# Sixteen down-projection tiles with the low part's first tokens appended to the high part's matmul

## The chip, the core and the metric

The kernel runs on one core of one Trainium2 chip. The metric is the device time of one execution in microseconds (us), the median of several runs; less is better.

## The reference

One inference step of a two-layer decoder trunk over 256 prompt tokens and 8 sample tokens (264 token columns), model width 2048, all in float32. Layer 0 mixes tokens with a Conformer convolution module, layer 1 with a gated linear recurrence (HGRN2); behind each mixer stands a channel mixer, and a last RMSNorm closes it. The change lies in the channel mixer of layer 0:

```python
def conv_ffn(x, buf, w_up, w_dw, b_dw, w_down):
    h = x @ w_up                                        # 2048 -> 2 * 5632
    h, new_buf = causal_depthwise_conv(h, buf, w_dw, b_dw)
    gate, up = jnp.split(h, 2, axis=-1)
    return (jax.nn.silu(gate) * up) @ w_down, new_buf   # 5632 -> 2048
...
        x = x + y
        h = rmsnorm(x, norm_ffn[i])
        y, s = conv_ffn(h, ffn_state[i], ffn_w_up[i], ffn_w_dw[i], ffn_b_dw[i], ffn_w_down[i])
        x = x + y
```

## The kernel before

Channels lie on the 128 partitions and the T = 264 tokens along the free axis. A product is computed in output tiles of 128 channels. TensorE holds a 128x128 weight block, streams the 128x264 activations of one block of input channels past it, and adds up over the k blocks in one PSUM bank (512 float32 per partition).

Nearly all products are done in three passes. The weights are cut by ScalarE into a high part `wh` and by VectorE into a low part `wl`, the activations likewise into a high and a low part, all of type float32r (the page prints it as f32 on TensorE); what is added up is high by high, `wh` by low, and `wl` by high. That is `step`: three matmuls of 264 columns for each k, at L179 (`wh`, high), L180 (`wh`, low) and L181 (`wl`, high). Each loads its own weight block. A product that is on the list `NATIVE` is done instead in plain float32 by one instruction for each k (L176), which the trace records as two matmuls.

The work is cut into slots, written out by hand and in a fixed order: `slot` issues the matmuls of one output tile on TensorE, and then what goes along with it on VectorE and ScalarE: work put off by `later` (the previous tile's addition to the residual stream `x` in `residual`, L278; the gating and convolution of up-projection tiles) and the split of the weights two tiles ahead (`split_hi` L137, `split_lo` L149). Weight tiles are loaded by DMA further ahead still; the raw weights, `wh` and `wl` have three buffers each, PSUM tiles five.

`conv_ffn` cuts the 5632 hidden channels into `CHUNKS` = 4 chunks of `FC` = 11 blocks of 128. For a chunk, `up` computes 22 up-projection tiles (16 blocks deep, so 48 matmuls each), and gates them into `gh` and `gl`, the high and the low part of 11 activation blocks; `down` computes 16 down-projection tiles `p_dn` (11 blocks deep, 33 matmuls each), and each is added to `x`. A chunk's down tiles run behind the next chunk's up tiles, except for the last chunk, whose down tiles follow at once. So the first chunk's down tiles of layer 0, 16 tiles and 528 matmuls, run from 611.3 to 675.8 us, between up-projection tiles.

Inside a down slot the second matmul reads `gl`, which VectorE has written as `gate - gh` (L587), long before.

Of the kernel before, what the change touches and what calls it, by code (L numbers as in the profile page):

```python
# [17 lines left out]
P = 128  # L18
# [13 lines left out]

# columns of the packed per-channel parameters
_FIELDS = [
# [8 lines left out]

# output tiles of the first two products that go through the four-pass float32 path
NATIVE = {("pw1", n) for n in range(2 * KT)} | {("pw2", 0), ("pw2", 1), ("ho", 0)}
AHEAD = 2
LOADS = 4
TE = 17
# the second mixer's products: gates wait, so that enough of them are left to stream beside the last head's scan
GATE_AFTER = (3, 4, 6, 7, 9, 10, 12, 13, 15)  # L50
# [10 lines left out]
def kernel(ctx: ExitStack, tc: tile.TileContext, a: dict):  # L61
# [11 lines left out]

# [1 line left out]
    xall = cp.tile([P, KT, T], F32, tag="x", name="x")  # L75
# [12 lines left out]

# [1 line left out]
    order = []  # L90
# [64 lines left out]

# [1 line left out]
    todo = [([], [], []) for _ in range(12)]  # L157

    def later(slots, fn, last=False, first=False):
        """Run fn in the slots-th slot from here: before the split of a coming weight tile, or after it."""  # L160
        todo[slots][0 if first else 2 if last else 1].append(fn)
# [10 lines left out]

    def step(pt, ww, k, last, rhs, full):
        wh, wl = ww
        if wl is None:
            pe.matmul(pt[:, :T], wh[:, k, :], full[k], start=(k == 0), stop=last)  # L176
            return
        rh, rl = rhs[k]
        pe.matmul(pt[:, :T], wh[:, k, :], rh, start=(k == 0), stop=False)  # L179
        pe.matmul(pt[:, :T], wh[:, k, :], rl, start=False, stop=False)  # L180
        pe.matmul(pt[:, :T], wl[:, k, :], rh, start=False, stop=last)  # L181

    def slot(keys, rhs, full=None, ahead=AHEAD):
        """One product (or a few, side by side) and the work that goes along with it."""
        upto("hi", split_hi, cnt["use"] + len(keys))
        upto("lo", split_lo, cnt["use"] + len(keys))
        pts = []
        for key in keys:
            assert order[cnt["use"]] == key, (order[cnt["use"]], key)
            cnt["use"] += 1  # L190
            pts.append((bank(f"p_{key[0]}_{key[1]}"), parts.pop(key)))
        upto("load", load, cnt["use"] - 1 + LOADS)
        for k in range(depth(keys[0])):
            for pt, ww in pts:
                step(pt, ww, k, k == depth(keys[0]) - 1, rhs, full)
        begin, early, late = turn()
        for fn in begin:
            fn()
        upto("hi", split_hi, cnt["use"] + ahead)
        for fn in early:  # L200
            fn()
        upto("lo", split_lo, cnt["use"] + ahead)
        for fn in late:
            fn()
        return [pt for pt, _ in pts]

# [1 line left out]
    def rsqrt_steps(y, v, t):  # L208
        """y = v ** -0.5 by Newton steps from a guess on the exponent's bits."""
        yi = y.bitcast(I32)  # L210
        yield vec.tensor_scalar(out=yi, in0=v.bitcast(I32), scalar1=1, scalar2=None, op0=ALU.arith_shift_right)
        yield vec.tensor_scalar(out=yi, in0=yi, scalar1=-1.0, scalar2=float(0x5F3759DF), op0=ALU.mult, op1=ALU.add)
        for _ in range(3):
            yield vec.tensor_tensor(out=t, in0=v, in1=y, op=ALU.mult)
            yield vec.scalar_tensor_tensor(out=t, in0=t, scalar=-0.5, in1=y, op0=ALU.mult, op1=ALU.mult)
            yield vec.scalar_tensor_tensor(out=y, in0=t, scalar=1.5, in1=y, op0=ALU.add, op1=ALU.mult)
# [5 lines left out]
    class Stats:  # L222
        """Sum of squares over the channels, a tile at a time; then 1/rms on every partition."""

# [46 lines left out]

    def residual(n, pt, st, hl, name, scale, bias=None):
        """x += product, in the next slot; and what the next product needs of it."""
        hold = {}

        def add():
            if bias is None:
                vec.tensor_tensor(out=x[n], in0=x[n], in1=pt[:, :T], op=ALU.add)  # L278
            else:
                vec.scalar_tensor_tensor(out=x[n], in0=pt[:, :T], scalar=bias, in1=x[n], op0=ALU.add, op1=ALU.add)  # L280
            if st is not None:
                hold["sq"] = st.square(x[n])
            if hl is not None:
                hl.append(high(n, x[n], name, scale(n)))
            elif st is not None:
                act.activation(x[n], x[n], AF.Identity, scale=pcol("norm_final", n))
# [9 lines left out]

    # lower bounds of the forget gates: softmax over the layers' axis, cumulated, less the first
    lb = cp.tile([P, KT], F32, tag="lb", name="lb")
# [13 lines left out]

    # ================= layer 0, mixer: Conformer convolution =================
    with ExitStack() as ph:
# [63 lines left out]

        # the last tile: TE of its taps on the tensor engine, as products with diagonal matrices
        diag = {}  # L380
# [14 lines left out]
        def taps(i, lo, hi):  # L395
            """Two sums, of every other tap: c[i], which the last tap opened, and part, with what is independent of it."""
            u, ci = m[i], c[i]
# [132 lines left out]

    # ================= channel mixer =================
    def conv_ffn(layer, hl, rs, scale):
        """scale: what the next product's operand is scaled with (None: no product follows)."""
        rstd = rs.y
        with ExitStack() as ph:
# [39 lines left out]
            def up(f):  # L575
                gh = fp.tile([P, T], F32R, tag="gh", name=f"gh{layer}_{f}", bufs=2 * FC)
                gl = fp.tile([P, T], F32R, tag="gl", name=f"gl{layer}_{f}", bufs=2 * FC)
                cg = half(f, "g")
# [7 lines left out]
                later(1, gate)  # L586
                later(1, lambda: vec.tensor_tensor(out=gl, in0=cu, in1=gh.bitcast(F32), op=ALU.subtract), last=True)  # L587
                return gh, gl

# [3 lines left out]
            def down(ch, g):  # L593
                end = ch == CHUNKS - 1
                for n in range(KT):
                    pt, = slot([(f"dn{layer}", ch * KT + n)], g)
                    residual(n, pt, st if end else None, nxt if end else None, f"after{layer}", scale)

# [13 lines left out]

    # ================= layer 1, mixer: HGRN2 =================
    with ExitStack() as ph:
# [11 lines left out]
        o2 = h1.tile([P, HEADS, T], F32, tag="o2", name="o2")  # L626
        # what a pair of neighbouring blocks of b tokens is scaled with: queries by (1, the first's gates), keys by (the second's, 1)
        G = {}
# [4 lines left out]
        def gated_by(b):  # L633
            """The gates of all blocks of b tokens, in their order."""
            at = G[b][:, 0, 0, 1:]
            n = SEQ // (2 * b)
            return bass.AP(at.tensor, at.offset, [at.ap[0], [2, n], [2 * n - 1, 2]])
# [28 lines left out]
        def doubling(h, lo, hi):  # L666
            """Products of the gates to a block's end, times the keys, and from its start, times the queries; it doubles."""
            d = heads[h]
# [36 lines left out]

        # the layer norm's 1/rms with tokens on partitions
        rtok = h1.tile([P, 3], F32, tag="rtok", name="rtok")
# [111 lines left out]
        def sample_state_and_norm(h):  # L819
            """By turns: neither waits for its last step, then."""  # L820
            for _ in zip_longest(sample_state(h), head_norm(h)):
                pass
# [31 lines left out]

        # the samples' norms: of all heads but the last, and of the last
        def sample_squares(lo, hi):
# [34 lines left out]
        def parted(last):  # L891
            """The output of the heads up to here in two parts, in buffers that the scan is done with."""
            lo, hi = len(ohl), last + 1
# [61 lines left out]

    # ================= final norm: the prompt's with tokens on partitions =================
    with ExitStack() as ph:
# [13 lines left out]
        for i in range(2):  # L971
            turn_back(i, 0, bank(f"p_y{i}_0"))
        # sums of squares: of the prompt's tokens on their partitions, of the samples' on every partition
        for i in range(3):
# [120 lines left out]
```

## Time and profile before

| what | before |
|---|---|
| median of 3 runs | 2487.59 us (2486.34 to 2487.78) |
| span of the profiled execution | 2484.5 us |
| TensorE matmul busy | 2460.8 us, 99% of the span |
| VectorE busy | 1762.4 us, 71% |
| ScalarE busy | 1109.1 us, 45% |
| mean granted TensorE clock | 0.997 |
| HBM traffic | 182 GB/s over the span |

How to read it: the profiled execution is given by its span, from the first to the last instruction of the core; the run list holds no time for that execution apart, and the median lies 3.1 us above the span, which is what lies around it (start and end of a launch). PE is TensorE's matmuls, PEld its weight loads, which run beside matmuls; DVE is VectorE and ACT is ScalarE. A matmul's duration in the rows runs from its start to a modelled end and overlaps the next matmul's; the distance from one start to the next is what a matmul costs.

### The profile page before, as it was taken

How to read it: one execution, taken by the hardware profiler on the slowest of the kernel's cores; microseconds unless marked ns; L12 is line 12 of the kernel's file. 1: busy time of each engine (PE TensorE's matmuls, PEld its weight loads, DVE VectorE, ACT ScalarE, POOL GpSimd, SP SyncE). 2: the span in 40 equal slices, each digit the busy share in tenths (PEclk: the TensorE clock that was granted, in tenths of full speed). 3: DMA queues.
4: the chain of work that ended last, by engine and by line, in shares of the span. 5: the costliest groups of instructions: out<-in, count | busy, mean ns of one | idle time of the engine just before them, and what ended most of it. 6: DMA issues, size and time to landing. Idle time of an engine off the chain costs nothing.

```text
span 2484.5 us, 46787 instructions
## 1 busy us (share of the span) xinstructions
PE 2460.8 (99%) x19879; PEld 2411.7 (97%) x19879; DVE 1762.4 (71%) x3098; ACT 1109.1 (45%) x1743; POOL 0.2 (0%) x4
## 2 busy tenths in 40 slices
PE   8999899999999999999999999999999999999998
PEld 7888899999999999999999999999999999999998
DVE  8999867676576566568877777767676656656655
ACT  1112645444344344345655565444444444434434
POOL 0000000000000000000000000000000000000000
PEclk9999999999999999999999999999999999999999
DMA  7443445544644554555555555455555455465453
GB/s 268 151 153 141 170 174 200 186 175 159 205 176 161 196 187 166 181 188 203 211 187 199 201 211 191 161 202 193 187 175 182 157 201 185 152 205 187 161 178 129
DMA packets 78129, 452.92 MB, mean 182 GB/s; under 512 B 8544, under 2 KB 13024, under 8 KB 39008
## 3 DMA queue, kind: packets, MB, share of 16 engines
q1 hardware_dynamic: 77920, 449.94, 51.4%
q8 instruction: 155, 2.54, 0.4%
q14 instruction: 54, 0.44, 0.0%
HBM read 436.31 MB, written 15.50 MB: 182 GB/s over the span
## 4 chain that ended last, share of the span: by engine, by line
PE 99%; DVE 1%; DMA 0%; ACT 0%; issue 0%; SPq 0%; ACTq 0%; DVEq 0%
PE p_up L181 14%; PE p_up L179 14%; PE p_up L180 14%; PE p_pw L176 10%; PE p_dn L181 7%; PE p_dn L180 7%; PE p_dn L179 7%; PE p_hi L179 1%; PE p_hf L179 1%; PE p_hq L179 1%; PE p_hf L181 1%; PE p_hi L180 1%; PE p_hq L181 1%; PE p_hi L181 1%; PE p_hq L180 1%; PE p_hf L180 1%
## 5 line engine op out<-in xcount | busy, mean ns | idle before, releaser
L179 PE MATMUL p_up<-h_ffn,wh_up 128*128 128x264 f32 x2816 | 801.0, 284 | 0.0
L181 PE MATMUL p_up<-h_ffn,wl_up 128*128 128x264 f32 x2816 | 800.7, 284 | 0.0
L180 PE MATMUL p_up<-l_ffn,wh_up 128*128 128x264 f32 x2816 | 797.6, 283 | 0.0
L149 DVE TENSOR_TENSOR wl_up<-w_up,wh_up 128x2048 fp32r<-128x2048 f32 x176 | 403.6, 2293 | 231.9 <-ACT wh_up L137 231.9
L137 ACT CAST wh_up<-w_up 128x2048 fp32r<-128x2048 f32 x176 | 335.9, 1909 | 505.7 <-PE p_up L180 446.8
L179 PEld LDWEIGHTS p_up<-h_ffn,wh_up 128*128 128x128 f32 x2816 | 530.1, 188 | 0.1
L181 PEld LDWEIGHTS p_up<-h_ffn,wl_up 128*128 128x128 f32 x2816 | 530.0, 188 | 0.0
L180 PEld LDWEIGHTS p_up<-l_ffn,wh_up 128*128 128x128 f32 x2816 | 529.7, 188 | 0.1
L181 PE MATMUL p_dn<-gh,wl_dn 128*128 128x264 f32 x1408 | 400.8, 285 | 0.0
L179 PE MATMUL p_dn<-gh,wh_dn 128*128 128x264 f32 x1408 | 400.3, 284 | 0.0
L180 PE MATMUL p_dn<-gl,wh_dn 128*128 128x264 f32 x1408 | 400.1, 284 | 0.0
L137 ACT CAST wh_dn<-w_dn 128x1408 fp32r<-128x1408 f32 x128 | 175.9, 1374 | 325.9 <-PE p_dn L180 243.8
L149 DVE TENSOR_TENSOR wl_dn<-w_dn,wh_dn 128x1408 fp32r<-128x1408 f32 x128 | 208.1, 1625 | 108.3 <-ACT wh_dn L137 108.3
L180 PEld LDWEIGHTS p_dn<-gl,wh_dn 128*128 128x128 f32 x1408 | 265.3, 188 | 0.0
L181 PEld LDWEIGHTS p_dn<-gh,wl_dn 128*128 128x128 f32 x1408 | 264.7, 188 | 0.0
L179 PEld LDWEIGHTS p_dn<-gh,wh_dn 128*128 128x128 f32 x1408 | 264.6, 188 | 0.0
L176 PE MATMUL p_pw<-xg,w_pw 128*128 128x264 f32 x960 | 213.9, 386 | 0.0
L176 PEld LDWEIGHTS p_pw<-xg,w_pw 128*128 128x128 f32 x960 | 182.4, 190 | 31.2
L567 DVE SCALAR_TENSOR_TENSOR C<-H,par,C 128x255 f32<-128x255 f32 x352 | 169.2, 481 | 6.3
L278 DVE TENSOR_TENSOR x<-x,p_dn 128x264 f32<-128x264 f32 x128 | 54.9, 429 | 111.9 <-PE p_dn L181 111.9
L561 DVE TENSOR_TENSOR H<-p_up,rstd_ffn 128x264 f32<-128x264 f32 x176 | 76.0, 432 | 78.2 <-PE p_up L181 78.2
L562 ACT ACTIVATE C<-H,par 128x264 f32<-128x264 f32 x176 | 105.5, 599 | 13.9 <-DVE H L561 13.9
(307 smaller groups left out, 4047.8 us busy)
## 6 DMA issues: line engine op xcount, KB each, us to landing
w_up<-in_up SPq DMA_DIRECT2D x176, 1024.0 KB
w_dn<-in_dn SPq DMA_DIRECT2D x128, 704.0 KB
w_pw<-in_pw SPq DMA_DIRECT2D x47, 1024.0 KB
w_hf<-in_hf SPq DMA_DIRECT2D x16, 1024.0 KB
w_hq<-in_hq SPq DMA_DIRECT2D x16, 1024.0 KB
w_hi<-in_hi SPq DMA_DIRECT2D x16, 1024.0 KB
w_hg<-in_hg SPq DMA_DIRECT2D x16, 1024.0 KB
w_ho<-in_ho SPq DMA_DIRECT2D x16, 1024.0 KB
```

What stands on the lines that cost most here:

```text
L137: act.copy(wh[:, :kk, :], raw[key][:, :kk, :])
L149: vec.tensor_tensor(out=wl[:, :kk, :], in0=raw.pop(key)[:, :kk, :], in1=wh.bitcast(F32)[:, :kk, :], op=ALU.subtract)
L176: pe.matmul(pt[:, :T], wh[:, k, :], full[k], start=(k == 0), stop=last)
L179: pe.matmul(pt[:, :T], wh[:, k, :], rh, start=(k == 0), stop=False)
L180: pe.matmul(pt[:, :T], wh[:, k, :], rl, start=False, stop=False)
L181: pe.matmul(pt[:, :T], wl[:, k, :], rh, start=False, stop=last)
L278: vec.tensor_tensor(out=x[n], in0=x[n], in1=pt[:, :T], op=ALU.add)
L561: vec.tensor_tensor(out=h, in0=pt[:, :T], in1=rstd, op=ALU.mult)
L562: act.activation(cc, h, AF.Identity, scale=wv[:, j, 2:3], bias=pcol("ffn_b", layer * 2 * FT + j))
L567: vec.scalar_tensor_tensor(out=cc[:, d:SEQ], in0=h[:, : SEQ - d], scalar=wv[:, j, 2 - d : 3 - d], in1=cc[:, d:SEQ], op0=ALU.mult, op1=ALU.add)
```

## The change

Of the 16 down tiles of chunk 0 in layer 0 (`WIDE_AT`), the first 8 get a width of 400, the last 8 of 512. `gh` and `gl` of one block now lie side by side in one tile `gb` of 528 columns, everywhere in both channel mixers. For a wide tile, the first matmul of each k streams the first `wide` columns of `gb` past `wh`: all 264 of the high part, and the first 136 (or 248) of the low part, whose products land in PSUM columns 264 and up. The second matmul is `wl` by the high part, as the third was before. The third is `wh` by the rest of the low part, 128 (or 16) columns, added onto PSUM columns 136 (or 248) to 263. The columns streamed for each k stay 792, and each k still has three matmuls, each with its own weight load. In `residual`, a second VectorE addition brings the products of PSUM columns 264 and up to `x`.

```diff
+WIDE = [400] * 8 + [512] * 8
+WIDE_AT = (0, 0)
...
-    def step(pt, ww, k, last, rhs, full):
+    def step(pt, ww, k, last, rhs, full, wide=0):
...
+        if wide:
+            both = rhs[k][2]
+            pe.matmul(pt[:, :wide], wh[:, k, :], both[:, :wide], start=(k == 0), stop=False)
+            pe.matmul(pt[:, :T], wl[:, k, :], both[:, :T], start=False, stop=False)
+            pe.matmul(pt[:, wide - T : T], wh[:, k, :], both[:, wide:], start=False, stop=last)
+            return
-        rh, rl = rhs[k]
+        rh, rl = rhs[k][:2]
...
                 vec.tensor_tensor(out=x[n], in0=x[n], in1=pt[:, :T], op=ALU.add)
+                if wide:
+                    rest = slice(0, wide - T)
+                    vec.tensor_tensor(out=x[n][:, rest], in0=x[n][:, rest], in1=pt[:, T:wide], op=ALU.add)
...
-                gh = fp.tile([P, T], F32R, tag="gh", name=f"gh{layer}_{f}", bufs=2 * FC)
-                gl = fp.tile([P, T], F32R, tag="gl", name=f"gl{layer}_{f}", bufs=2 * FC)
+                gb = fp.tile([P, 2 * T], F32R, tag="gb", name=f"gb{layer}_{f}", bufs=2 * FC)
+                gh, gl = gb[:, :T], gb[:, T:]
...
-                    pt, = slot([(f"dn{layer}", ch * KT + n)], g)
-                    residual(n, pt, st if end else None, nxt if end else None, f"after{layer}", scale)
+                    wide = WIDE[n] if (layer, ch) == WIDE_AT else 0
+                    pt, = slot([(f"dn{layer}", ch * KT + n)], g, wide=wide)
+                    residual(n, pt, st if end else None, nxt if end else None, f"after{layer}", scale, wide=wide)
```

What stands on TensorE at the start of the first down tile, two of its eleven k: before,

```order
L179 MATMUL p_dn0_0_5615<-gh0_0_2705,wh_dn0_0_5536 128x264
L180 MATMUL p_dn0_0_5615<-gl0_0_2706,wh_dn0_0_5536 128x264
L181 MATMUL p_dn0_0_5615<-gh0_0_2705,wl_dn0_0_5545 128x264
L179 MATMUL p_dn0_0_5615<-gh0_1_2843,wh_dn0_0_5536 128x264
L180 MATMUL p_dn0_0_5615<-gl0_1_2844,wh_dn0_0_5536 128x264
```

and now, where the first of each three is 400 columns wide, `wl` has moved from third place to second, and 128 columns are left for the third:

```order
L184 MATMUL p_dn0_0_5593<-gb0_0_2705,wh_dn0_0_5514 128x400
L185 MATMUL p_dn0_0_5593<-gb0_0_2705,wl_dn0_0_5523 128x264
L186 MATMUL p_dn0_0_5593<-gb0_0_2705,wh_dn0_0_5514 128x128
L184 MATMUL p_dn0_0_5593<-gb0_1_2842,wh_dn0_0_5514 128x400
L185 MATMUL p_dn0_0_5593<-gb0_1_2842,wl_dn0_0_5523 128x264
```

In both, the three matmuls of one k alternate between two weight blocks, so no two neighbours share one. From tile 8 on the widths are 512, 264 and 16.

What stands on VectorE in the same place (additions to `x`, splits of coming weight tiles into `wl`, the last `gl` of the second chunk): before,

```order
L278 TENSOR_TENSOR x_69<-x_69,p_dn0_0_5615 128x264
L149 TENSOR_TENSOR wl_dn0_3_5706<-w_dn0_3_5616,wh_dn0_3_5698 128x1408
L587 TENSOR_TENSOR gl0_21_5484<-C0_65_5614,gh0_21_5483 128x264
L278 TENSOR_TENSOR x_69<-x_69,p_dn0_1_5662 128x264
L149 TENSOR_TENSOR wl_dn0_4_5748<-w_dn0_4_5663,wh_dn0_4_5745 128x1408
```

and now:

```order
L288 TENSOR_TENSOR x_69<-x_69,p_dn0_0_5593 128x264
L291 TENSOR_TENSOR x_69<-x_69,p_dn0_0_5593 128x136
L153 TENSOR_TENSOR wl_dn0_3_5685<-w_dn0_3_5594,wh_dn0_3_5676 128x1408
L600 TENSOR_TENSOR gb0_21_5462<-C0_65_5592,gb0_21_5462 128x264
L288 TENSOR_TENSOR x_69<-x_69,p_dn0_1_5640 128x264
L291 TENSOR_TENSOR x_69<-x_69,p_dn0_1_5640 128x136
```

One addition of 136 (later 248) columns stands behind each of 16 others and ahead of the split of a coming weight tile; nothing else has moved.

More of the change, by code (lines that the diff above doesn't have):

```diff
@@ L181, in step, with slot @@
         pe.matmul(pt[:, :T], wl[:, k, :], rh, start=False, stop=last)
-    def slot(keys, rhs, full=None, ahead=AHEAD):
+    def slot(keys, rhs, full=None, ahead=AHEAD, wide=0):
         upto("hi", split_hi, cnt["use"] + len(keys))
@@ L194, in slot @@
             for pt, ww in pts:
-                step(pt, ww, k, k == depth(keys[0]) - 1, rhs, full)
+                step(pt, ww, k, k == depth(keys[0]) - 1, rhs, full, wide)
         begin, early, late = turn()
@@ L270, in low, with residual @@
         return h, lo
-    def residual(n, pt, st, hl, name, scale, bias=None):
+    def residual(n, pt, st, hl, name, scale, bias=None, wide=0):
         hold = {}
@@ L586, in up @@
                 later(1, gate)
-                later(1, lambda: vec.tensor_tensor(out=gl, in0=cu, in1=gh.bitcast(F32), op=ALU.subtract), last=True)
-                return gh, gl
+                later(1, lambda: vec.tensor_tensor(out=gl, in0=cu, in1=gb.bitcast(F32)[:, :T], op=ALU.subtract), last=True)
+                return gh, gl, gb
             st = Stats(f"after{layer}", apart=scale is None)
```

## The prediction

> **What bounds the kernel now.** I read the page from the top: the engines' busy time, then the chain that ended last, then TensorE's own waits, and last the stretch in which the changed tiles run.
>
> ```profile
> span 2484.5 us, 46787 instructions
> PE 2460.8 (99%) x19879; PEld 2411.7 (97%) x19879; DVE 1762.4 (71%) x3098; ACT 1109.1 (45%) x1743; POOL 0.2 (0%) x4
> PE 99%; DVE 1%; DMA 0%; ACT 0%; issue 0%; SPq 0%; ACTq 0%; DVEq 0%
> PE p_pw L176 <- DMA w_pw<-in_pw: 7.3, 1, 7.3
> PE p_pw L176 <- ACT c L512: 6.8, 1, 6.8
> PE p_taps L393 <- DVE u L372: 1.2, 1, 1.2
> PE p_y L967 <- ACT y L995: 1.0, 1, 1.0
> ```
>
> TensorE is the bound: 99% of the chain is its matmuls, and its waits for others are the four rows quoted, 16.3 us together (engine and line, what it waited for, us in total, times, the longest). The first three lie in layer 0's mixer, ahead of the changed tiles; only the last, 1.0 us in the final norm, lies behind them. So a microsecond that TensorE gains or loses in the down tiles has next to nothing to be absorbed in, and reaches the end.
>
> The stretch itself, by time windows (start and end, length, busy time and count; granted clock, DMA share, GB/s; the first row is the tile `p_dn` on PE alone, the second all engines, PE, PEld, DVE, ACT, POOL):
>
> ```profile
> 611.33:675.75 64.42, 64.42 (x528) 1.00 0.56 189
> 611.30:676.00 64.70, 64.70 (x532) 64.70 (x531) 35.73 (x38) 24.45 (x21) 0.00 (x0) 1.00 0.56 190
> ```
>
> 528 matmuls in 64.42 us: 122.0 ns from one to the next, without a gap, at a granted clock of 1.00. Three of them, one k of one tile, cost 366.0 ns. VectorE works 35.73 us of 64.70, ScalarE 24.45, DMA is at 0.56.
>
> **What a matmul of another width costs.** Everything hangs on what those 122.0 ns consist of: time that goes with the columns, a fixed part, or the weight load that runs beside it. The timeline at the start of the stretch (start us, duration us):
>
> ```profile
> 611.33 0.29 PE L179 MATMUL p_dn<-gh,wh_dn 128*128 128x264 f32 x1
> 611.33 0.19 PEld L180 LDWEIGHTS p_dn<-gl,wh_dn 128*128 128x128 f32 x1
> 611.46 0.28 PE L180 MATMUL p_dn<-gl,wh_dn 128*128 128x264 f32 x1
> 611.46 0.19 PEld L181 LDWEIGHTS p_dn<-gh,wl_dn 128*128 128x128 f32 x1
> 611.58 0.28 PE L181 MATMUL p_dn<-gh,wl_dn 128*128 128x264 f32 x1
> ```
>
> The weights of the next matmul start to load when the matmul before it starts to stream, and not earlier: one weight block is loaded ahead, no more. So a matmul costs the longer of its own streaming and the load of its successor's weights, and I need both prices.
>
> *The load.* The nearest rows are the plain float32 products of one column, where nothing streams, and some others:
>
> ```profile
> 1187.18:1188.97 1.79, 1.79 (x16) 1.00 0.78 183
> L798 PEld LDWEIGHTS pos<-qks,sm x256: 190/192/192, 1187.0 to 1591.3; 128*128 128x128 f32 x128
> L739 PEld LDWEIGHTS pl<-R x640: 138/138/138, 1157.0 to 1561.7; 128*64 128x64 f32 x160
> L180 PEld LDWEIGHTS p_dn<-gl,wh_dn 128*128 128x128 f32 x1408 | 265.3, 188 | 0.0
> ```
>
> In the first row (L798 alone) 16 matmuls of one column follow each other every 1.79 / 16 = 0.112 us: that is the load of 128 weight columns. The recorded load time (the middle one of min/median/max) follows the weight columns, 192 ns for 128 and 138 for 64, and is 188 in the float32r down tiles. So I take it that a float32r block loads as slowly as a float32 one: 112 ns. Lower is not likely by more than those 4 ns; higher it can't be than 122, since the 264-column matmuls keep that pace.
>
> *The streaming.* Plain float32 has rows of other widths (each record streams twice, in two passes):
>
> ```profile
> L176 PE MATMUL p_pw<-xg,w_pw 128*128 128x264 f32 x960 | 213.9, 386 | 0.0
> L393 PE MATMUL p_taps<-u,diag 128*128 128x226 f32 x2 | 0.5, 354 | 0.0
> 99.73 1.08 PEld L176 LDWEIGHTS p_pw<-xg,w_pw 128*128 128x128 f32 x5
> ```
>
> From 226 to 264 columns the duration grows by 386 - 354 = 32 ns, 0.842 ns a column for two passes, 0.421 for one. Five loads of those products take 1.08 us, the last of them 0.19: (1.08 - 0.19) / 4 = 222.5 ns each, which is 264 x 0.842 = 222.3 with nothing fixed on top, the 112 ns load hidden beneath. For float32r, 264 x 0.421 = 111.1 ns, and measured are 122.0: 10.9 ns more. No row has float32r of another width, so these 10.9 ns are bounded. Low end: they come only because streaming and load are equally long there (111 and 112 ns) and disturb each other, and a wide matmul is free of them. High end: they go with the columns, 122.0 / 264 = 0.462 ns each. I take the value between, 10.9 ns fixed for each matmul that streams longer than its successor loads, since neither row decides.
>
> The Trainium skill, "TensorE: Matmul & The Clock Gate", section "Back-to-back issue gap", puts the distance of matmuls at N/2.4 + 2.5 ns at the full clock. By that the 264-column matmul would take 112.5 ns; the trace has 122.0, so the measurement decides here, and with 169.2 and 215.8 ns for the wide ones the sum would be that of the low end.
>
> **The sum.** One k before: 3 x 122.0 = 366.0 ns. After, in the new order: a wide matmul (beneath it the load of `wl`), 264 columns of `wl` (beneath it the load of `wh`; 122.0 as now), and a narrow one, 128 or 16 columns, whose streaming of 54 or 7 ns is shorter than the load of the next k's `wh`, so it costs 112.
>
> - 400 wide: 400 x 0.421 + 10.9 = 179.3; 179.3 + 122.0 + 112 = 413.3 ns, +47.3.
> - 512 wide: 215.6 + 10.9 = 226.5; 226.5 + 122.0 + 112 = 460.5 ns, +94.5.
> - 8 tiles of 11 k each: 88 x (47.3 + 94.5) ns = 12.5 us.
> - Low end: 168.4 and 215.6 for the wide ones, 402.4 and 449.6 ns: 88 x (36.4 + 83.6) = 10.6 us.
> - High end: 0.462 a column, 184.8 and 236.5, and 122.0 for the narrow ones, 428.8 and 480.5 ns: 88 x (62.8 + 114.5) = 15.6 us.
>
> In one sentence: the columns are the same 792, but the long matmul has nothing to hide for its last 60 to 110 ns, and the short one no longer hides a load.
>
> **The rest costs nothing, and this is the cover:**
>
> ```profile
> 612.81 1.63 DVE L149 TENSOR_TENSOR wl_dn<-w_dn,wh_dn 128x1408 fp32r<-128x1408 f32 x1 [0.85 <-ACT wh_dn L137]
> L278 DVE TENSOR_TENSOR x<-x,p_dn 128x264 f32<-128x264 f32 x128 | 54.9, 429 | 111.9 <-PE p_dn L181 111.9
> L569 DVE TENSOR_TENSOR C<-C,pre 128x8 f32<-128x8 f32 x176 | 28.1, 160 | 0.0
> ```
>
> The 16 second additions: between 160 ns for 8 columns and 429 for 264, so 295 for 136 and 412 for 248, 8 x 0.295 + 8 x 0.412 = 5.7 us on VectorE, which idles 64.70 - 35.73 = 29 us in this stretch. Behind each waits the split of a coming weight tile. The one at 612.81 us is for the third tile and is done at 614.44; that tile starts two tiles later, 611.33 + 2 x 33 x 0.122 = 619.4. So a delay of 0.4 us meets a margin of 5.0, and slower tiles widen it. That `wl` is needed one matmul earlier takes 0.1 us from the same margin; that `wh` is read to the tile's last matmul frees its buffer 0.1 us later, against ScalarE's idle 40 us here. The PSUM tile is held 0.4 us longer, of five. Laying `gh` and `gl` in one tile adds no instruction; every block is finished a whole chunk of up tiles before its down tiles, or 16 down tiles before in the last chunk. DMA: the same transfers, in a stretch that gets longer.
>
> So the profiled span would go from 2484.5 to 2497.0, and the median, 3.1 us above the span, from 2487.6 to 2500.1. A measurement of this kernel can tell about 0.2% (5.0 us) from no change; +12.5 is 0.5%.
>
> **Rivals.**
>
> *Not slower: loads run further ahead.* If TensorE could fetch two weight blocks ahead, the idle 60 to 110 ns beneath the wide matmul would take up the load of the third. Then only columns and fixed parts count, 792 x 0.421 + 3 x 10.9 = 366 ns as before: 0 us, 2487.6. If the disturbance went too, loads alone would bound, 3 x 112 = 336: -30 ns x 176 = -5.3 us, 2482.3. It decides from the point where the narrow matmul costs less than about 65 ns beside 400 and 17 beside 512. For it: nothing in the rows. Against it: in the timeline each load starts with the preceding matmul and not before. The Trainium skill's same section speaks for it: for a sustained stream of load and matmul it gives 81 ns at N=128 and 131 at N=512, with loads pulled ahead through the queue. By that the three would cost what three of 264 cost; the 112 ns of the one-column row contradicts the 81.
>
> *Narrow float32r is slower.* All float32r rows have 264 columns; a matmul of 128 or 16 might need more passes.
>
> ```profile
> L798 PE MATMUL pos<-qks,sm 128*128 128x1 f32 x256 | 29.5, 245 | 0.0
> ```
>
> Plain float32 does: 16 heads of 8 one-column products, 128, stand as 256 records, so 2 x 112 = 224 ns each. Were all narrow ones done so, 112 ns more on 176 of them: 19.7 us on top, +32.2, 2519.8. Were they streamed four times with one load, 128 columns would take 4 x 128 x 0.421 = 215.6, 16 columns stay under the load: 88 x 103.6 ns = 9.1 on top, +21.6, 2509.2. Against it: plain float32 keeps its price per column from 264 down to 226 without a step.
>
> *VectorE's second addition is not covered.* Then a tile start waits for it: 5.7 us on top, +18.2, 2505.8. Against it the 5.0 us margin.
>
> **How the numbers follow.** Load-bound narrow matmuls as summed: 0.76. Narrow ones dearer still: 0.13, of which 0.08 for the cheaper form. Addition uncovered: 0.04. Loads further ahead: 0.07, of which 0.05 no change and 0.02 faster. The time is the first case's, 2500.1. Its own bounds are 2498.2 to 2503.2; down to 2495.5 it has room for a load of 108 and a little more, and the range goes up to 2510 to take in the uncovered addition and the cheaper form of dear narrow matmuls: 0.71 + 0.04 + 0.07. Slower is 0.76 + 0.13 + 0.04 = 0.93, same 0.05, faster 0.02.
>
> **What would show it.** In the profile after, the stretch from 611.3 us should hold the same 528 matmuls in about 64.4 + 12.5 = 76.9 us: 8 tiles of 4.55 us (11 x 413.3) and 8 of 5.07 (11 x 460.5). The load behind a narrow matmul and that matmul should be 112 ns apart from the next load, and loads beneath wide ones should come early and wait. If the stretch still takes 64 us, loads run ahead; if the 128-column tiles are slower than the 16-column ones, or records double, narrow float32r is dear; if PE shows waits for `wl_dn` or `x`, the additions cost. All other stretches should keep their length; a change there would mean that the joined tile `gb` matters, which I have at nothing.

## The result, and the profile after

The changed kernel takes 2500.59 us (median of 3, 2500.38 to 2500.84) against 2487.59: 13.0 us or 0.5% slower, ratio 1.0054, 95% interval 1.0034 to 1.0074. Its profiled execution has a span of 2498.6 us. The page, the changed stretch by time windows (the whole, all engines; then the 8 tiles of width 400 and the 8 of width 512 on PE alone), and PE's waits:

```profile
span 2498.6 us, 46803 instructions
PE 2474.9 (99%) x19879; PEld 2423.1 (97%) x19879; DVE 1768.0 (71%) x3114; ACT 1109.1 (44%) x1743; POOL 0.2 (0%) x4
PE 99%; DVE 1%; DMA 0%; ACT 0%; issue 0%; SPq 0%; ACTq 0%; DVEq 0%
611.64:689.03 77.39, 77.39 (x530) 73.58 (x529) 41.17 (x52) 24.21 (x20) 0.00 (x0) 1.00 0.48 160
611.64:648.26 36.62, 36.62 (x265) 1.00 0.45 146
648.26:689.03 40.77, 40.77 (x266) 1.00 0.50 173
PE p_pw L180 <- DMA w_pw<-in_pw: 7.3, 1, 7.3
PE p_pw L180 <- ACT c L525: 6.8, 1, 6.8
PE p_taps L406 <- DVE u L385: 1.2, 1, 1.2
PE p_y L981 <- ACT y L1009: 1.0, 1, 1.0
```

TensorE still carries 99% of the chain, with the same number of records (19879) and the same four waits, now at other line numbers. The 16 tiles take 77.39 us where they took 64.42: the 13.0 us are here. A tile of width 400 takes 36.62 / 8 = 4.58 us and one of 512 takes 5.10, where 4.55 and 5.07 were forecast. PEld is no longer busy throughout (73.58 of 77.39): beneath the long matmuls it has nothing to do. The granted clock is 1.00 as before.

Where inside a k, the timeline shows (start us, duration us): a 400-wide tile above, a 512-wide one below.

```profile
614.32 0.28 PE L185 MATMUL p_dn<-gb,wl_dn 128*128 128x264 f32 x1
614.32 0.19 PEld L186 LDWEIGHTS p_dn<-gb,wh_dn 128*128 128x128 f32 x1
614.44 0.22 PE L186 MATMUL p_dn<-gb,wh_dn 128*128 128x128 f32 x1
614.44 0.19 PEld L184 LDWEIGHTS p_dn<-gb,wh_dn 128*128 128x128 f32 x1
614.50 0.39 PE L184 MATMUL p_dn<-gb,wh_dn 128*128 128x400 f32 x1
614.55 0.19 PEld L185 LDWEIGHTS p_dn<-gb,wl_dn 128*128 128x128 f32 x1
614.73 0.28 PE L185 MATMUL p_dn<-gb,wl_dn 128*128 128x264 f32 x1
...
653.77 0.17 PE L186 MATMUL p_dn<-gb,wh_dn 128*128 128x16 f32 x1
653.77 0.19 PEld L184 LDWEIGHTS p_dn<-gb,wh_dn 128*128 128x128 f32 x1
653.79 0.48 PE L184 MATMUL p_dn<-gb,wh_dn 128*128 128x512 f32 x1
653.88 0.19 PEld L185 LDWEIGHTS p_dn<-gb,wl_dn 128*128 128x128 f32 x1
654.11 0.28 PE L185 MATMUL p_dn<-gb,wl_dn 128*128 128x264 f32 x1
```

Here one has to read the load rows, not the matmul rows. The wide matmul behind a narrow one is recorded early (614.50, or 653.79), but its weights began to load only at 614.44 (653.77) and it can't stream before they are there: its record is longer by the wait (478 ns on average for 512 columns, against 396 in the swapped order below, where the wide matmul doesn't wait). As in the prediction's timeline, a load starts when the matmul before its own starts to stream, so the distance from one load to the next is what the matmul in between really costs. Averaged over the 88 k of each width (start to start of the loads, ns):

```
                     wide    264 columns   narrow    sum     before
400 / 264 / 128      186.8      121.6       108.3    416.7    366.1
512 / 264 / 16       234.6      120.9       108.2    463.7    366.1
```

88 x (50.6 + 97.6) ns = 13.0 us. A narrow matmul costs 108 ns whether it has 128 columns or 16.

### The profile page after: what moved, and what is told of

It is laid out like the page before. It is cut to its first block, busy times and chain, and to the rows that moved or that the text cites. A ratio compares the mean times of both kernels' runs of the same rounds, so it can differ in the third digit from the quotient of the medians.

```text
span 2498.6 us, 46803 instructions
## 1 busy us (share of the span) xinstructions
PE 2474.9 (99%) x19879; PEld 2423.1 (97%) x19879; DVE 1768.0 (71%) x3114; ACT 1109.1 (44%) x1743; POOL 0.2 (0%) x4
## 4 chain that ended last, share of the span: by engine, by line
PE 99%; DVE 1%; DMA 0%; ACT 0%; issue 0%; SPq 0%; ACTq 0%; DVEq 0%
PE p_up L191 14%; PE p_up L189 14%; PE p_up L190 14%; PE p_pw L180 10%; PE p_dn L189 6%; PE p_dn L191 6%; PE p_dn L190 6%; PE p_dn L184 2%; PE p_hi L189 1%; PE p_hf L189 1%; PE p_hq L189 1%; PE p_hf L191 1%; PE p_hq L191 1%; PE p_hi L190 1%; PE p_hi L191 1%; PE p_hq L190 1%
## 5 line engine op out<-in xcount | busy, mean ns | idle before, releaser
L189 PE MATMUL p_dn<-gb,wh_dn 128*128 128x264 f32 x1232 | 353.9, 287 | 0.0
L191 PE MATMUL p_dn<-gb,wl_dn 128*128 128x264 f32 x1232 | 350.1, 284 | 0.0
L190 PE MATMUL p_dn<-gb,wh_dn 128*128 128x264 f32 x1232 | 350.1, 284 | 0.0
L190 PEld LDWEIGHTS p_dn<-gb,wh_dn 128*128 128x128 f32 x1232 | 233.5, 190 | 0.0
L191 PEld LDWEIGHTS p_dn<-gb,wl_dn 128*128 128x128 f32 x1232 | 232.9, 189 | 0.0
L189 PEld LDWEIGHTS p_dn<-gb,wh_dn 128*128 128x128 f32 x1232 | 231.3, 188 | 0.0
```

## The experiments

Six kernels were run, each beside runs of the kernel before on the same chip (its medians there were 2487.09 and 2486.81 us). Theory L is the prediction's: a narrow matmul costs its successor's weight load, a wide one its streaming, the rest is free.

**Only the joined tile.**

```diff
-WIDE = [400] * 8 + [512] * 8
+WIDE = [0] * 16
```

> Only the layout of the change is left: high and low part lie in one joined tile, every down tile runs as three matmuls of 264 columns as before. Theory L (a narrow matmul costs the 109 ns load of its successor's weights, the rest of the change is free): no change, within 1 us of the kernel before, 2487.6 us. Rival J (the joined tile costs): part of the 13 us stays, 3 us or more above before.

Measured 2488.02 us, ratio 1.0003 (0.9994 to 1.0011). The stretch, tile `p_dn` on PE:

```profile
611.72:676.14 64.42, 64.42 (x528) 1.00 0.56 189
```

64.42 us, as before: in the changed tiles the layout costs nothing. Elsewhere it costs a little. The later down tiles of layer 0, chunk 1 and then chunks 2 and 3 together, all with three matmuls of 264 columns, before and below it with the joined tile:

```profile
804.39:868.71 64.32, 64.32 (x528) 1.00 0.55 190
997.35:1126.10 128.75, 128.75 (x1056) 1.00 0.56 188
```

```profile
804.77:869.30 64.53, 64.53 (x528) 1.00 0.55 189
997.93:1126.89 128.96, 128.96 (x1056) 1.00 0.56 188
```

Each of these two stretches is 0.21 us longer, and so are the same two of layer 1: 0.8 us in all, which the spread of the runs hides from the medians. The changed kernel has the same lengths there (64.54 and 128.96). What makes the difference was not tried.

**All down tiles 288 wide.**

```diff
-WIDE = [400] * 8 + [512] * 8
-WIDE_AT = (0, 0)
+WIDE = [288] * 16
+WIDE_AT = [(l, c) for l in range(2) for c in range(CHUNKS)]
...
-                    wide = WIDE[n] if (layer, ch) == WIDE_AT else 0
+                    wide = WIDE[n] if (layer, ch) in WIDE_AT else 0
```

> All 128 down tiles of both layers 288 wide, so 240 columns for the third matmul: everything of the change but the narrow matmul, eight times as often. Theory L: the third matmul streams 240 x 0.46 = 111 ns, just above the 109 ns load, so the three cost 366 ns as before: within 3 us of before, 2485 to 2491 us. Rival J (the cost comes with the wide form as such): the change's 13 us times 8, about 2590 us; in part, if in part.

Measured 2487.1 us, ratio 1.0000 (0.9991 to 1.0009), and in the first chunk:

```profile
612.13:676.58 64.45, 64.45 (x528) 1.00 0.57 189
```

The whole form of the change (the new order of the three matmuls, overlapping accumulation in PSUM, the second addition, 128 of them) stands in this kernel eight times over, and costs nothing as long as the third matmul has 240 columns. Rival J is out: the form doesn't cost the 13 us, the widths do. The second additions have only 24 columns here, so the prediction's rival of an uncovered addition is settled elsewhere: in the changed kernel TensorE has no wait for `x`, `p_dn` or `wl_dn` among its four, and the 400-wide tiles of the half-weights kernel below, with additions of 136 columns, take the time before.

**A ladder of widths.** The same places, and

```diff
-WIDE = [400] * 8 + [512] * 8
+WIDE = [272 + 16 * n for n in range(16)]
```

> The sixteen tiles of each of the eight chunks get sixteen widths, 272 to 512 in steps of 16 (narrow ones of 256 down to 16 columns): a price list. Theory L: the narrow one costs its own streaming, 0.46 ns a column, down to 236 columns (109 ns), and 108 to 109 flat below; wide ones grow with the columns, 125 to 235 ns. So the three cost 366 ns as before up to a width of 288, then 0.46 ns more for every column. Sum over the widths 750 ns for one k of all sixteen, times 88: 66 us above before (60 to 75), 2548 to 2563 us. Rival J (joined tile, second addition, earlier use of the low weights cost): extra time at 272 and 288 too. Rival N (narrow float32r is dear below some width): a jump at that width.

Measured 2552.07 us, ratio 1.0263 (1.0244 to 1.0281): 65.3 us. Seven of the sixteen tiles of the first chunk, of widths 272, 288, 304, 320, 336, 400 and 512 (a window of one tile is one row; 4.03 us was a tile before):

```profile
611.42:615.43 4.01, 4.01 (x33) 1.00 0.14 52
615.43:619.45 4.02, 4.02 (x35) 1.00 0.49 179
619.45:623.56 4.11, 4.11 (x35) 1.00 0.54 175
623.56:627.72 4.16, 4.16 (x35) 1.00 0.53 177
627.72:631.97 4.25, 4.25 (x35) 1.00 0.54 175
645.19:649.76 4.57, 4.57 (x35) 1.00 0.43 154
678.75:683.86 5.11, 5.11 (x36) 1.00 0.60 202
```

Free at 272 and 288, then every 16 columns cost more. The distances of the loads over all eight chunks (ns), for seven wide matmuls and the narrow one of each (of the narrow ones without the last k of a tile):

```
wide      272    288    304    320    336    400    512
costs   125.8  134.5  142.9  149.7  157.6  186.5  234.4
narrow    256    240    224    208    192    128     16
costs   117.3  110.2  108.6  108.6  108.6  108.5  108.4
```

The narrow price falls with the columns down to 240 and is flat at 108.3 to 109.4 for all fourteen widths from 224 to 16. There is no jump anywhere, so the rival of dear narrow float32r (N) is out. Wide matmuls grow by (234.4 - 125.8) / 240 = 0.4525 ns a column.

**The narrow matmul beside the same weights.** In the changed kernel's 16 tiles, the last two of the three change places:

```diff
             pe.matmul(pt[:, :wide], wh[:, k, :], both[:, :wide], start=(k == 0), stop=False)
-            pe.matmul(pt[:, :T], wl[:, k, :], both[:, :T], start=False, stop=False)
-            pe.matmul(pt[:, wide - T : T], wh[:, k, :], both[:, wide:], start=False, stop=last)
+            pe.matmul(pt[:, wide - T : T], wh[:, k, :], both[:, wide:], start=False, stop=False)
+            pe.matmul(pt[:, :T], wl[:, k, :], both[:, :T], start=False, stop=last)
```

> The changed tiles with the order wide, narrow, 264 columns of the low weights: now wide and narrow use the same weight block one after the other. Theory L, each matmul loads its own block and only one block ahead: the narrow matmul again covers the next load (now of the low weights) badly, the same 13 us above before, 2500.6 us. Rival S, an equal block is not loaded again, or loads run ahead by two: the load of the low weights starts beneath the wide matmul, and the cost is 0 to 3 us, 2488 to 2491 us. In the trace L has 108 to 109 ns from the narrow matmul's successor's load to the next load.

Measured 2500.76 us, ratio 1.0056 (1.0042 to 1.0070), the change's own time. The loads of one k of a 512-wide tile, and the first load of the next:

```profile
655.11 0.19 PEld L184 LDWEIGHTS p_dn<-gb,wh_dn 128*128 128x128 f32 x1
655.24 0.19 PEld L185 LDWEIGHTS p_dn<-gb,wh_dn 128*128 128x128 f32 x1
655.47 0.19 PEld L186 LDWEIGHTS p_dn<-gb,wl_dn 128*128 128x128 f32 x1
655.58 0.19 PEld L184 LDWEIGHTS p_dn<-gb,wh_dn 128*128 128x128 f32 x1
```

From the load of `wl` to the next load are 108.4 ns on average behind the 400-wide matmuls and 108.6 behind the 512-wide ones. The narrow matmul's block equals the one in use, and still has a load of its own (L185), as long in the record as the others. The load of `wl` (L186) does not start beneath the wide matmul, although nothing else is loaded there for over 70 ns. This is the prediction's rival of loads that run further ahead, and it is out.

**Half the weights behind the narrow matmul.** On top of the swapped order:

```diff
-            pe.matmul(pt[:, :T], wl[:, k, :], both[:, :T], start=False, stop=last)
+            m = P if last else 64
+            pe.matmul(pt[:m, :T], wl[:, k, :m], both[:, :T], start=False, stop=last)
```

> As the swapped order, but in ten of eleven k the low weights' matmul takes only 64 of the 128 weight columns (half of that product is left out), still streaming 264 columns. So the matmul that follows the narrow one has half the weights to load. Theory L: the narrow one costs 54 ns in place of 108 (the load of 64 columns by the float32 rows), 160 x 54 ns = 8.7 us less than the swapped order, 2491.9 us. Rival O (108 ns is a narrow float32r matmul's own least time, whatever loads beside it): the same as the swapped order, 2500.6 us.

Measured 2491.85 us, ratio 1.0021 (1.0012 to 1.0030): 8.9 us under the swapped order. Its 400-wide and 512-wide tiles, below those of the swapped order, and a piece of its timeline:

```profile
612.08:648.72 36.64, 36.64 (x265) 1.00 0.45 148
648.72:689.72 41.00, 41.00 (x265) 1.00 0.48 170
```

```profile
611.61:643.84 32.23, 32.23 (x264) 1.00 0.49 164
643.84:680.57 36.73, 36.73 (x265) 1.00 0.56 193
```

```profile
655.30 0.17 PE L185 MATMUL p_dn<-gb,wh_dn 128*128 128x16 f32 x1
655.31 0.14 PEld L187 LDWEIGHTS p_dn<-gb,wl_dn 128*64 128x64 f32 x1
655.33 0.32 PE L187 MATMUL p_dn<-gb,wl_dn 128*64 128x264 f32 x1
655.36 0.19 PEld L184 LDWEIGHTS p_dn<-gb,wh_dn 128*128 128x128 f32 x1
```

The same narrow matmul of 16 columns, with 64 weight columns to load behind it, now costs 55.3 ns (80 k; 655.31 to 655.36), where it cost 108.6. With 128 columns it costs 58.9, a little more: there its own streaming has become the longer. So 108 ns was never the narrow matmul's own time (rival O is out); it is the load of 128 weight columns, and 55 that of 64. The 400-wide tiles are back at 32.23 us, the time before, since in ten of eleven k hardly any load is left uncovered there.

**Without the narrow matmul.** The third `pe.matmul` line of the wide form is dropped, and `stop=last` moves to the second.

> The narrow matmul is left out (the high weights by the last 128 or 16 low columns of the 16 changed tiles are missing from the sum). Theory L: its whole 108 ns go and nothing else: a wide matmul of 186.8 or 234.6 and one of 121.5 ns remain, 308 and 356 ns against 366 before: 88 x (58 + 10) = 6.0 us below before, 2481.6 us. If wide matmuls delay what comes behind them by more than their own streaming, as they would if the accumulation of overlapping columns were what costs, it is less of a gain, or none.

Measured 2479.76 us, ratio 0.9972 (0.9961 to 0.9983). The two halves of the stretch, again on PE:

```profile
610.94:637.55 26.61, 26.61 (x176) 1.00 0.60 198
637.55:668.38 30.83, 30.83 (x178) 1.00 0.64 221
```

57.44 us, 7.0 less than before, where I expected 6.0: the wide matmuls cost 181.4 and 230.7 ns here, against 186.8 and 234.6 in the changed kernel. So the wide matmul that follows a load-bound narrow one is itself 4 to 5 ns dearer. The swapped order points the same way: there the 264-column matmul follows the narrow one and costs 124.3 in place of 121.2, while the wide one falls to 183.4 and 233.3. A small delay, then, seems to fall on whichever matmul comes behind a wait for weights. Its size is uncertain by some 2 ns and its cause was not tried: in the joined kernel's first chunk, where nothing waits, the first, second and third matmul of a k average 123.4, 122.0 and 120.6 ns.

## Why the prediction was right

- *The bound and where the time shows.* TensorE's time reached the end undiminished: 13.0 us in the stretch, 13.0 between the medians. The profiled span grew by 14.1: besides the 13.0 there are 0.8 us in the later down tiles, which the joined tile alone brings too and the prediction had at nothing, and 0.3 ahead of the stretch, whose start lies anywhere from 610.94 to 612.13 us in the eight traces. So it is in part chance that the medians differ by the stretch's 13.0 alone; the three runs of the kernel before spread over 1.4 us.
- *One load ahead, so a short matmul costs the next load.* Right, and shown three ways: flat price from 224 columns down, no load ahead in the swapped order, and half the price for half the weights.
- *The load: taken at 112 ns, measured 108.3.* I took the pace of the one-column float32 products and set the 4 ns between the recorded load times (192 and 188) aside; the measured price is lower by nearly as much: 176 x 3.7 ns = 0.7 us too much. The Trainium skill, "TensorE: Matmul & The Clock Gate", section "LDWEIGHTS (loading the stationary operand)", gives a load as its columns divided by 1.2, 106.7 ns for 128 and 53.3 for 64, whatever the rows; the trace's 108.4 and 55.3 lie 2 ns above both.
- *The streaming: 10.9 ns fixed taken, of bounds from none to 0.462 ns a column.* This was the term most off: the wide ones cost 186.8 and 234.6, not 179.3 and 226.5, 1.4 us too little, and at the high end of what I had for 400 columns, even 2 ns above it. Of that, 4 to 5 ns are the delay behind a narrow matmul, which the sum did not have. What is left, 181.4 and 230.7 in the kernel without the narrow matmul, grows by 0.44 ns a column, and from 264 columns on by 0.43 to 0.45, as one compares with the joined kernel's 123.4 or with the 121.0 and 119.6 beside the wide ones. That is more than the 0.421 that the prediction took from plain float32, so the surplus goes partly with the columns.
- *The 264-column matmul: 122.0 taken, 121.6 and 120.9 measured*, 0.1 us.
- The two larger errors have opposite signs, 1.4 - 0.7 - 0.1 = 0.6 us, which is why 12.5 came so near to 13.0. The time was better than its terms.
- *The additions and waits at nothing.* Right: 296 and 411 ns each (295 and 412 had been put between two rows), beneath VectorE's idle time, no new wait on PE, and the 400-wide tiles with half the weights take the time before (32.23 against 32.21 us) with the same additions.

```profile
L291 DVE TENSOR_TENSOR x<-x,p_dn 128x248 f32<-128x248 f32 x8 | 3.3, 411 | 0.3
L291 DVE TENSOR_TENSOR x<-x,p_dn 128x136 f32<-128x136 f32 x8 | 2.4, 296 | 0.3
```

## What to carry to other kernels

With as many matmuls and columns as before, moving columns from one matmul to another wins next to nothing here (4.01 us for the 272-wide tile, 4.03 before) and soon loses: each costs the longer of its own streaming and the next one's weight load, and equal widths above that load (240 float32r columns on 128 weight columns) waste neither. Before reshaping a stream of matmuls, read the price of a weight load off a place where little streams, and price every matmul against the load behind it. Where PE waits for weights, read the distances of the load records: the matmul records then start early and run long.

## What the runs showed of the hardware that I had not expected

- Float32r streams at about 0.44 ns a column on top of a few ns (121.0, 181.4 and 230.7 ns for 264, 400 and 512 columns), against 0.421 for half of a plain float32 record's price (222.5 ns for 264 columns), at the same granted clock of 1.00. The columns from 400 to 512 cost that too ((230.7 - 181.4) / 112 = 0.44), when the load of 108 ns beneath is over, so it is not the load beside it.
- A matmul that had to wait for its weights costs some 3 to 5 ns more than one of its width that had not (186.8 against 181.4, 234.6 against 230.7, 124.3 against 121.2), besides the wait.
- Two neighbouring matmuls on the same weight block have a load each (the swapped order, 188 ns in the record), and the load behind them starts no earlier for it.
